# The lead-in of a hybrid attention and SSM layer: x transposed once, three weight slices behind the first adaLN pair

## The chip, the core and the metric

The kernel runs on one NeuronCore of one Trainium2 chip. The metric is device time in microseconds. Before the change the median of three runs was 1358.09 us (1357.22 to 1360.01).

## The reference

One layer of a streaming encoder for two groups of frames that share their weights: 512 new frames of a prompt and 64 frames of a sample (a cache of 512 keys stands before these). Only the start matters here:

```python
mod = (jax.nn.silu(c) @ w_ada + b_ada)[:, None, :]          # w_ada: 1024 x 6144
sh1, sc1, gt1, sh2, sc2, gt2 = jnp.split(mod, 6, axis=-1)
h = rms_normalize(x) * g_norm_mix * (1.0 + sc1) + sh1       # x: 576 x 1024
q, k, v, qi, ki, wi, z, xbc, dt, gate_logits = jnp.split(h @ w_in, offs, axis=-1)
```

Everything else (sparse attention with an indexer, a Mamba-2 scan, the merge of both branches, a SwiGLU FFN) comes from h @ w_in and from x itself, which is needed again for the residual.

## The kernel before

**Layout.** h is kept transposed, model channels on the 128 partitions: eight tiles (kt = 0 to 7) of 128 channels by 576 frames (512 of the prompt, 64 of the sample). Matmuls are made of three products of fp32r halves: a high part (`hTh`, `wh`) and a low part (`hTl`, `wl`), high times high, low times high, high times low. A weight slice of 512 KB is loaded to `raw` (two buffers), split by ScalarE into `wh` and by VectorE into `wl` (three buffers each).

**The lead-in.** x comes in five blocks of up to 128 frames (`xt`). ScalarE squares each with a sum over the row; 1/rms follows on VectorE and GpSimd (`rs`). VectorE scales the block (`xn`), TensorE transposes it with the identity in eight pieces (`px<-ident,xn`), ScalarE copies it to `xnT`. Apart from this, TensorE also transposes x itself (`mm<-ident,xt`), VectorE copies that to `xs`, and it is stored to `x_d` for the residual.

The adaLN shift and scale come in four pairs (`ada_pair`): pair j loads 256 columns of shift and 256 of scale weights (four loads of 512 KB, `adr`, eight buffers), and TensorE makes two groups of 32 small matmuls (`py<-adr,sil`), one per half of the model channels. The result is copied (`ra`), transposed, given its bias (`modc`) and made into A1 = (1 + scale) * g. Then `h_tile` makes two tiles of h: `hu` = xnT * A1 + shift (even tiles on VectorE, odd ones on ScalarE), `hTh` a copy of hu on ScalarE, `hTl` = hu - hTh (VectorE, for two tiles GpSimd).

Three weight slices are used while h comes into being: one called misc (104 columns: indexer keys, head weights, dt; its product is in an `mm` buffer with 104 columns) and two gate slices (an `mm` buffer, and the two halves in `px` and `py`). For each tile of h there are six matmuls with each. The first full weight use behind them is the first indexer query projection, `mm<-wh,hTh` with 256 columns, whose two slices are the fourth and fifth.

**What sets the order.** The program is written in its natural order and recorded as a list of operations. A planner (`Plan.order`) gives each a cost in time and a priority, its place in the program less an offset (`R.prio`), and runs a list schedule: the engine that is free first takes the ready operation with the lowest priority number. The instructions are then emitted in that order on each engine. All lines of the profile are therefore one line, 534, and work is told apart by tile names. Each load is issued on SyncE's queue (SP), in the planned order; the program uses eight DMA semaphores in turn, so that a load waits for the one eight places ahead of it. `EARLY` says how many weight slices may have been asked for after each pair.

Of the kernel before, what the change touches and what calls it, by code (L numbers as in the profile page):

```python
# [248 lines left out]
class Plan:  # L249
# [142 lines left out]
    def order(self):  # L392
# [50 lines left out]
        while n < len(ops):  # L443
# [98 lines left out]
def build(tc, I, O):  # L542
# [74 lines left out]
    def fetch(done, limit=1 << 30):  # L617
# [6 lines left out]
        with R.prio(4000 if done or limit > 99 else 0):  # L624
            more = True
            while more:
                more = False
                j = state["ld"]
                if j < min(len(queue), limit) and j < state["sp"] + NRAW:
                    i, s = queue[j]  # L630
                    if s == "misc":
                        raw = wp.tile([P, 8, 104], F32, name="rawm", tag="raw", bufs=NRAW)
# [3 lines left out]
                    else:  # L636
                        raws[j] = (load_raw(*s), s[1], s[2], 27 <= j < 48)
# [184 lines left out]
    pool.memset(rs, 1.0)  # L822
    for tb in range(5):
# [11 lines left out]
    rowsD = sp.tile([48, P], F32, name="rowsD")  # L835
    sync.dma_start(rowsD, I["b_ada"][0].rearrange("(a b) -> a b", b=P))
    badc = cp.tile([P, 48], F32, name="badc")
    t = px("pbadc")
    pe.transpose(t[:, :48], rowsD, ident[:48, :48])
    vec.tensor_copy(badc, t[:, :48])  # L840
    rowsA = sp.tile([64, P], F32, name="rowsA")
    for r0, n, src in ((0, 8, I["g_norm_mix"][0]), (8, 8, I["g_norm_ffn"][0]), (16, 16, I["g_ssm_norm"][0]), (32, 32, I["b_conv"][0])):
        sync.dma_start(rowsA[r0:r0 + n], src.rearrange("(a b) -> a b", b=P))
# [43 lines left out]
    with R.prio(-1500):  # L887
        for tb in range(5):
# [1300 lines left out]
```

## Time and profile before

| | |
|---|---|
| median of 3 runs | 1358.09 us |
| the profiled execution, its own time | 1358.19 us |
| span from first to last instruction | 1356.4 us |
| mean granted TensorE clock | 0.999 |
| TensorE busy | 1335.1 us, 98% |
| VectorE, ScalarE, GpSimd busy | 1130.7, 737.3, 241.5 us |
| loaded and stored | 200.02 MB, 147 GB/s in the mean |

A row of the timeline gives start and length in us, engine, operation, and what is written from what; in square brackets the idle time of the engine before it and what ended this. A matmul's length is from its start to its modelled end, so neighbours overlap, and the distance of their starts is what one costs. PE is TensorE, PEld its weight loads, DVE VectorE, ACT ScalarE, POOL GpSimd, SP and SPq SyncE with its queue.

### The profile page before, as it was taken

The page shows a single profiled execution, that of the slowest core. Times are in us where ns is not written, and L with a number is a line of the kernel's source. Part 1 is how long each engine was busy: PE and PEld are TensorE (multiplying, and loading weights), DVE is VectorE, ACT ScalarE, POOL GpSimd, SP SyncE. Part 2 cuts the span into 40 slices and gives each one's busy share as a digit, 9 for nine tenths or more (in the row PEclk, how much of TensorE's full clock was granted, in tenths as well). Part 3 has the DMA queues.
Part 4 walks back from the last instruction along what each step waited for, and adds up shares of the span by engine and source line. Part 5 has one row for each costly group of instructions (what it writes and reads, how often), then busy time and mean ns, then how long its engine had stood idle before and what let it go on. Part 6 is the DMA issues. An engine that isn't in the chain of part 4 may idle for free.

```text
span 1356.4 us, 27609 instructions
## 1 busy us (share of the span) xinstructions
PE 1335.1 (98%) x10651; PEld 1298.5 (96%) x10651; DVE 1130.7 (83%) x2238; ACT 737.3 (54%) x1515; POOL 241.5 (18%) x370
## 2 busy tenths in 40 slices
PE   7999999999999999999999999999999999999998
PEld 5899999999999999999999999999999999999998
DVE  4688999887777798888887688858799998868997
ACT  5445343787777666666565342225576555564543
POOL 1212011230301235545453300001000000000000
PEclk9999999999999999999999999999999999999999
DMA  9862335674754464455445698748333433334423
GB/s 292 235 176 88 101 115 140 142 176 116 165 143 119 131 185 114 115 149 136 135 112 175 212 300 252 232 143 260 98 94 110 125 103 89 98 101 130 133 73 87
DMA packets 268370, 200.02 MB, mean 147 GB/s; under 512 B 25168, under 2 KB 240368, under 8 KB 268240
## 3 DMA queue, kind: packets, MB, share of 16 engines
q1 hardware_dynamic: 264288, 184.11, 46.4%
q0 software_dynamic: 3952, 14.16, 5.1%
q8 instruction: 83, 1.36, 0.4%
q14 instruction: 47, 0.39, 0.1%
HBM read 158.27 MB, written 28.96 MB: 138 GB/s over the span
## 4 chain that ended last, share of the span: by engine, by line
PE 82%; DVE 10%; DMA 3%; ACT 1%; issue 1%; POOL 1%; SPq 1%; DVEq 0%; ACTq 0%; POOLq 0%
PE mm L534 56%; PE py L534 14%; PE px L534 11%; DVE score L534 3%; DVE m L534 2%; DVE wl L534 2%; DMA raw<-in_w_in 1%; SPq L534 1%; DMA xt<-in_x_sample 1%; DMA raw<-in_w_down 0%; ACT wh L534 0%; DMA rawb<-in_w_down 0%; DMA rowsB<-in_w_conv 0%; DVE cu L534 0%; DVE tok L534 0%
## 5 line engine op out<-in xcount | busy, mean ns | idle before, releaser
L534 ACT ACTIVATE wh<-raw 128x1024 fp32r<-128x1024 f32 (+3 forms) x146 | 142.3, 978 | 182.5 <-PE mm L534 125.8
L534 PE MATMUL mm<-hTh,wh 128*128 128x288 f32 (+1 forms) x1024 | 230.3, 302 | 0.5 <-ACT hTh L534 0.5
L534 PE MATMUL mm<-hTl,wh 128*128 128x288 f32 (+1 forms) x1024 | 230.7, 300 | 0.0
L534 PE MATMUL mm<-hTh,wl 128*128 128x288 f32 (+1 forms) x1024 | 229.2, 300 | 0.5 <-DVE wl L534 0.5
L534 PEld LDWEIGHTS mm<-hTh,wh 128*128 128x128 f32 (+1 forms) x1024 | 165.8, 188 | 4.0 <-ACT hTh L534 1.3
L534 PEld LDWEIGHTS mm<-hTl,wh 128*128 128x128 f32 (+1 forms) x1024 | 166.4, 188 | 2.4 <-issue 0.9
L534 PEld LDWEIGHTS mm<-hTh,wl 128*128 128x128 f32 (+1 forms) x1024 | 165.1, 188 | 2.5 <-issue 1.1
L534 DVE TENSOR_TENSOR wl<-raw,wh 128x1024 fp32r<-128x1024 f32 (+2 forms) x102 | 123.4, 1211 | 28.5 <-ACT wh L534 24.3
L534 DVE SCALAR_TENSOR_TENSOR cu<-xc,wc,cu 128x579 f32<-128x579 f32 x96 | 83.2, 868 | 2.0 <-ACT cu L534 1.0
L534 PE MATMUL mm<-wh,hTl 128*128 128x256 f32 x256 | 72.6, 284 | 0.0
L534 PE MATMUL mm<-wl,hTh 128*128 128x256 f32 x256 | 72.1, 282 | 0.0
L534 PE MATMUL mm<-wh,hTh 128*128 128x256 f32 x256 | 71.9, 283 | 0.0
L534 DVE SCALAR_TENSOR_TENSOR aacc<-adr,sil,aacc 128x512 f32<-128x512 f32 x84 | 59.1, 752 | 4.3 <-DMA adr<-in_w_ada 4.3
L534 PE MATMUL mm<-yh,wl 128*128 128x288 f32 x256 | 55.2, 296 | 0.0
L534 PE MATMUL mm<-yh,wh 128*128 128x288 f32 x256 | 55.0, 296 | 0.0
L534 PE MATMUL mm<-yl,wh 128*128 128x288 f32 x256 | 54.9, 296 | 0.0
L534 PE MATMUL mm<-xhS,wh 128*128 128x290 f32 (+1 forms) x248 | 54.7, 295 | 0.0
L534 ACT ACTIVATE P<-lg,mn 128x128 f32<-128x128 f32 (+4 forms) x72 | 41.8, 581 | 23.5 <-DVE mn L534 22.1
L534 PE MATMUL mm<-xhS,wl 128*128 128x290 f32 (+1 forms) x232 | 51.1, 295 | 0.0
L534 ACT ACTIVATE dec<-dec,nacs 128x128 f32<-128x128 f32 x128 | 42.4, 393 | 15.4 <-POOL dec L534 15.4
L534 PEld LDWEIGHTS mm<-wh,hTl 128*128 128x128 f32 x256 | 48.4, 189 | 0.4
L534 PEld LDWEIGHTS mm<-wh,hTh 128*128 128x128 f32 x256 | 48.0, 188 | 0.6 <-issue 0.4
(553 smaller groups left out, 3993.2 us busy)
## 6 DMA issues: line engine op xcount, KB each, us to landing
raw<-in_w_in SPq DMA_DIRECT2D x80, 512.0 KB, 4.0
adr<-in_w_ada SPq DMA_DIRECT2D x36, 512.0 KB, 5.1
raw<-in_w_gate_up SPq DMA_DIRECT2D x22, 512.0 KB, 4.0
wl<-raw POOLq DMA_DIRECT2D x21, 512.0 KB, 5.1
rawu<-in_w_gate_up SPq DMA_DIRECT2D x20, 512.0 KB, 3.9
bc<-acs_d SPq DMA_DIRECT2D x32, 256.0 KB, 3.4
raw<-in_w_branch_ssm SPq DMA_DIRECT2D x16, 512.0 KB, 4.9
gate_d<-sg SPq DMA_DIRECT2D x16, 288.0 KB, 2.1
```

The source lines that it names most:

```text
L534: getattr(engines[x.eng], x.fn)(*[real(a) for a in x.args], **{k: real(v) for k, v in x.kw.items()})
```

## The change

- x itself is transposed as each block comes in, into `xT` (576 frames by 8 tiles); nine of the ten copies are on VectorE, one on ScalarE. `x_d` is stored from `xT`, in four stores.
- 1/rms is transposed and spread over the partitions by TensorE (five transposes of a broadcast column), and VectorE multiplies `xT` by it to give `xnT`, in five products. The scaled blocks `xn`, their 40 transposes and their copies are gone.
- The bias rows and gain rows (`rowsD`, `rowsA`) are transposed while x still comes in.
- The first three weight slices have raw buffers of their own, and `EARLY` asks for all three behind pair 0; the fourth is asked for after pair 3.
- `h_tile`: ScalarE makes hTh straight from xnT (scale and shift in the same instruction, in two parts); VectorE makes hu and hTl for all tiles.
- In the planner, the load rate of SyncE's queue in the first 60 us is 335 in place of 360 (thousand bytes per us), and the first seven weight loads have no priority offset.

```diff
-                dma_free = max(queue + 1.3, dma_free) + op.bytes / 360e3
+                dma_free = max(queue + 1.3, dma_free) + op.bytes / (335e3 if at < 60.0 else 360e3)
...
-    def load_raw(src, nk, n):
-        raw = wp.tile([P, nk, n], F32, name=f"raw{cnt[0]}", tag="raw", bufs=NRAW)
+    def load_raw(src, nk, n, own=0):
+        if own:
+            raw = sp.tile([P, nk, n], F32, name=f"rawe{cnt[0]}_{own}")
+        else:
+            raw = wp.tile([P, nk, n], F32, name=f"raw{cnt[0]}", tag="raw", bufs=NRAW)
...
-                if j < min(len(queue), limit) and j < state["sp"] + NRAW:
+                if j < min(len(queue), limit) and (j < 3 or j < max(state["sp"], 3) + NRAW):
                     i, s = queue[j]
+                    at = R.offset
+                    R.offset = 0 if j < 7 else at
...
+    xT = xsp.tile([P, 8, T], F32, name="xT")
     for tb in range(5):
         n = P if tb < 4 else NS
+        p = pmm(f"pxt{tb}")
+        for kt in range(8):
+            pe.transpose(p[:, kt // 4, (kt % 4) * P:(kt % 4) * P + n], xt[tb][:n, kt * P:(kt + 1) * P], ident[:n, :n])
         xn = sp.tile([P, D], F32, name=f"xn{tb}", tag="xn", bufs=2)
         act.activation(xn[:n], xt[tb][:n], AF.Square, accum_out=rs[:n, tb:tb + 1])
         rstd_of(rs[:n, tb:tb + 1], rs[:n, tb:tb + 1], 1, n, D)
-        vec.tensor_scalar(xn[:n], xt[tb][:n], rs[:n, tb:tb + 1], None, op0=OP.mult)
         for k4 in range(2):
-            p = px(f"pxn{tb}_{k4}")
-            for j in range(4):
-                kt = 4 * k4 + j
-                pe.transpose(p[:, j * P:j * P + n], xn[:n, kt * P:(kt + 1) * P], ident[:n, :n])
-            act.activation(xnT[:, 4 * k4:4 * k4 + 4, tb * P:tb * P + n], p.rearrange("p (k q) -> p k q", k=4)[:, :, :n], AF.Copy)
+            d, src = xT[:, 4 * k4:4 * k4 + 4, tb * P:tb * P + n], p[:, k4].rearrange("p (k q) -> p k q", k=4)[:, :, :n]
+            if 2 * tb + k4 in (1,):
+                act.activation(d, src, AF.Copy)
+            else:
+                vec.tensor_copy(d, src)
...
+    pr = px("prs"), pairs_bank[:, 2 * P:3 * P]
+    for tb in range(5):
+        pe.transpose(pr[tb // 4][:, tb % 4 * P:tb % 4 * P + P], rs[:, tb:tb + 1].to_broadcast([P, P]), ident)
+    vec.tensor_tensor(xnT[:, 0:2, 0:NP_], xT[:, 0:2, 0:NP_], pr[0][:, None, :].to_broadcast([P, 2, NP_]), OP.mult)
+    vec.tensor_tensor(xnT[:, :, NP_:T], xT[:, :, NP_:T], pr[1][:, None, :NS].to_broadcast([P, 8, NS]), OP.mult)
+    for k in range(2, 8, 2):
+        vec.tensor_tensor(xnT[:, k:k + 2, 0:NP_], xT[:, k:k + 2, 0:NP_], pr[0][:, None, :].to_broadcast([P, 2, NP_]), OP.mult)
...
         for s, c0, n in PARTS:
-            if kt % 2:
-                act.activation(u[:, c0:c0 + n], xnT[:, kt, c0:c0 + n], AF.Identity, bias=sh1[:, kt, s:s + 1], scale=A1[:, kt, s:s + 1])
-            else:
-                vec.tensor_scalar(u[:, c0:c0 + n], xnT[:, kt, c0:c0 + n], A1[:, kt, s:s + 1], sh1[:, kt, s:s + 1], op0=OP.mult, op1=OP.add)
-        act.activation(hTh[:, kt, :], u, AF.Copy)
-        (pool if kt % 4 == 1 else vec).tensor_tensor(hTl[:, kt, :], u, hTh[:, kt, :].bitcast(F32), OP.subtract)
-
-    EARLY = [1, 2, 3, 3]
+            act.activation(hTh[:, kt, c0:c0 + n], xnT[:, kt, c0:c0 + n], AF.Identity, bias=sh1[:, kt, s:s + 1], scale=A1[:, kt, s:s + 1])
+            vec.tensor_scalar(u[:, c0:c0 + n], xnT[:, kt, c0:c0 + n], A1[:, kt, s:s + 1], sh1[:, kt, s:s + 1], op0=OP.mult, op1=OP.add)
+        vec.tensor_tensor(hTl[:, kt, :], u, hTh[:, kt, :].bitcast(F32), OP.subtract)
+
+    EARLY = [3, 3, 3, 4]
...
-    with R.prio(-1500):
-        for tb in range(5):
...
+    for hf in range(2):
+        xst.append((x_d[:, :, hf, 0:HP], xT[:, :, HP * hf:HP * hf + HP]))
+        xst.append((x_d[:, :, hf, HP:TH], xT[:, :, NP_ + HS * hf:NP_ + HS * hf + HS]))
```

Three places of the planned order show what moves. The first is SyncE's queue from pair 1 on; before (adr_4 to adr_7 at the top are pair 1, the next four pair 2, the last four pair 3; the 128x8x128 slices are the two gate slices, 128x4x256 the first one of the query projection):

```order
L534 DMA adr_6_167<-in_w_ada 128x4x256
L534 DMA adr_7_168<-in_w_ada 128x4x256
L534 DMA raw_1_85<-in_w_in 128x8x128
L534 DMA adr_0_161<-in_w_ada 128x4x256
L534 DMA adr_1_162<-in_w_ada 128x4x256
L534 DMA adr_2_163<-in_w_ada 128x4x256
L534 DMA adr_3_164<-in_w_ada 128x4x256
L534 DMA raw_1_85<-in_w_in 128x4x256
L534 DMA raw_0_84<-in_w_in 128x8x128
L534 DMA adr_4_165<-in_w_ada 128x4x256
L534 DMA adr_5_166<-in_w_ada 128x4x256
L534 DMA adr_6_167<-in_w_ada 128x4x256
```

and now, from the end of pair 0:

```order
L534 DMA adr_3_160<-in_w_ada 128x4x256
L534 DMA rawm_0_165<-in_w_in 128x8x72
L534 DMA rawm_0_165<-in_w_in 128x8x32
L534 DMA rawe1_1_0_166<-in_w_in 128x8x128
L534 DMA rawe2_2_0_167<-in_w_in 128x8x128
L534 DMA adr_4_161<-in_w_ada 128x4x256
```

The gate slices have moved ahead of pair 1; the query slice stands behind pair 3, where it was ahead of it.

The second is ScalarE between the end of x's part and the first h tiles, before (raw_0 to wh_0 is the misc slice):

```order
L534 ACTIVATE wh_0_86<-raw_0_84 128x832
L534 ACTIVATE xnT_0_153<-px_0_97 128x4x64
L534 ACTIVATE xnT_0_153<-px_1_98 128x4x64
L534 ACTIVATE hu_1_170<-xnT_0_153,modc_0_74,A1_0_117 128x512
L534 ACTIVATE hu_1_170<-xnT_0_153,modc_0_74,A1_0_117 128x64
L534 ACTIVATE hTh_0_131<-hu_0_169 128x576
```

and now:

```order
L534 ACTIVATE wh_0_84<-rawm_0_165 128x832
L534 ACTIVATE wh_1_85<-rawe1_1_0_166 128x1024
L534 ACTIVATE hTh_0_131<-xnT_0_149,modc_0_74,A1_0_117 128x512
L534 ACTIVATE hTh_0_131<-xnT_0_149,modc_0_74,A1_0_117 128x64
L534 ACTIVATE wh_2_86<-rawe2_2_0_167 128x1024
L534 ACTIVATE hTh_0_131<-xnT_0_149,modc_0_74,A1_0_117 128x512
```

The high part of the first h tile no longer waits for hu, and stands behind the split of the second slice; the third slice's split stands between the first two h tiles.

The third is TensorE behind the last adaLN group (`mm` with wh_1 and wl_1 is the first gate slice, `px` and `py` with wh_2 and wl_2 the second), before:

```order
L534 MATMUL mm_0_99<-hTh_0_131,wl_1_90 128x288 x2
L534 MATMUL mm_0_99<-hTh_0_131,wh_1_87 128x288 x2
L534 MATMUL mm_0_99<-hTl_0_132,wh_1_87 128x288 x2
L534 MATMUL py_1_96<-ident_0_71,ra_1_108 128x128
L534 MATMUL mm_0_99<-hTh_0_131,wl_1_90 128x288 x2
L534 MATMUL py_0_95<-hTh_0_131,wl_2_91 128x288
L534 MATMUL px_0_97<-ident_0_71,rowsB_0_159 128x128
L534 MATMUL px_1_98<-hTh_0_131,wh_2_88 128x288
```

and now:

```order
L534 MATMUL mm_1_98<-hTh_0_131,wl_0_87 104x288 x2
L534 MATMUL mm_0_97<-hTl_0_132,wh_1_85 128x288 x2
L534 MATMUL mm_0_97<-hTh_0_131,wl_1_88 128x288 x2
L534 MATMUL py_1_96<-ident_0_71,ra_1_108 128x128
L534 MATMUL mm_0_97<-hTh_0_131,wh_1_85 128x288 x2
L534 MATMUL mm_0_97<-hTl_0_132,wh_1_85 128x288 x2
L534 MATMUL px_0_99<-ident_0_71,rowsB_0_155 128x128
L534 MATMUL mm_0_97<-hTh_0_131,wl_1_88 128x288 x2
L534 MATMUL py_0_95<-hTl_0_132,wh_2_86 128x288
```

Between this group and the query projection stand 75 matmuls of the three slices before and 68 now; the rowsB transpose comes after 9 of them before and after 10 now.

More of the change, by code (lines that the diff above doesn't have):

```diff
@@ L636, in fetch @@
                     else:
-                        raws[j] = (load_raw(*s), s[1], s[2], 27 <= j < 48)
+                        raws[j] = (load_raw(*s, own=j if j < 3 else 0), s[1], s[2], 27 <= j < 48)
+                    R.offset = at
                     state["ld"] += 1
@@ L822, in build @@
     pool.memset(rs, 1.0)
+    rowsD = sp.tile([48, P], F32, name="rowsD")
+    rowsA = sp.tile([64, P], F32, name="rowsA")
+    badc = cp.tile([P, 48], F32, name="badc")
+    vc = cp.tile([P, 64], F32, name="vc")
+    sync.dma_start(rowsD, I["b_ada"][0].rearrange("(a b) -> a b", b=P))
+    for r0, n, src in ((0, 8, I["g_norm_mix"][0]), (8, 8, I["g_norm_ffn"][0]), (16, 16, I["g_ssm_norm"][0]), (32, 32, I["b_conv"][0])):
+        sync.dma_start(rowsA[r0:r0 + n], src.rearrange("(a b) -> a b", b=P))
+    xT = xsp.tile([P, 8, T], F32, name="xT")
     for tb in range(5):
         n = P if tb < 4 else NS
+        p = pmm(f"pxt{tb}")
+        for kt in range(8):
+            pe.transpose(p[:, kt // 4, (kt % 4) * P:(kt % 4) * P + n], xt[tb][:n, kt * P:(kt + 1) * P], ident[:n, :n])
         xn = sp.tile([P, D], F32, name=f"xn{tb}", tag="xn", bufs=2)
@@ L835, in build @@
[L835 to L843, printed above, removed]
+            d, src = xT[:, 4 * k4:4 * k4 + 4, tb * P:tb * P + n], p[:, k4].rearrange("p (k q) -> p k q", k=4)[:, :, :n]
@@ new lines, in build @@
+            if 2 * tb + k4 in (1,):
+                act.activation(d, src, AF.Copy)
+            else:
+                vec.tensor_copy(d, src)
+        if tb == 2:
+            t = px("pv")
+            pe.transpose(t[:, 0:48], rowsD, ident[:48, :48])
+            pe.transpose(t[:, 64:128], rowsA, ident[:64, :64])
+            vec.tensor_copy(badc, t[:, 0:48])
+            vec.tensor_copy(vc, t[:, 64:128])
+    pr = px("prs"), pairs_bank[:, 2 * P:3 * P]
+    for tb in range(5):
+        pe.transpose(pr[tb // 4][:, tb % 4 * P:tb % 4 * P + P], rs[:, tb:tb + 1].to_broadcast([P, P]), ident)
@@ L847, in build @@
-    t = px("pv")
-    pe.transpose(t[:, :64], rowsA, ident[:64, :64])
-    vec.tensor_copy(vc, t[:, :64])
     g_mix, g_ffn = vc[:, 0:8], vc[:, 8:16]
@@ L886, in build @@
     xst = []
-    with R.prio(-1500):
-        for tb in range(5):
-            n = P if tb < 4 else NS
-            p = pmm(f"pxt{tb}")
-            for kt in range(8):
-                pe.transpose(p[:, kt // 4, (kt % 4) * P:(kt % 4) * P + n], xt[tb][:n, kt * P:(kt + 1) * P], ident[:n, :n])
-            st = xsp.tile([P, 8, P], F32, name=f"xs{tb}", tag="xs", bufs=5)
-            for k4 in range(2):
-                vec.tensor_copy(st[:, 4 * k4:4 * k4 + 4, :n], p[:, k4].rearrange("p (k q) -> p k q", k=4)[:, :, :n])
-            if tb < 4:
-                xst.append((x_d[:, :, tb // 2, tb % 2 * P:tb % 2 * P + P], st))
-            else:
-                for hf in range(2):
-                    xst.append((x_d[:, :, hf, HP:TH], st[:, :, HS * hf:HS * hf + HS]))
+    for hf in range(2):
+        xst.append((x_d[:, :, hf, 0:HP], xT[:, :, HP * hf:HP * hf + HP]))
+        xst.append((x_d[:, :, hf, HP:TH], xT[:, :, NP_ + HS * hf:NP_ + HS * hf + HS]))
     sync.dma_start(rowsB, I["w_conv"][0].rearrange("j (a b) -> (j a) b", b=P))
```

3 lines of the change are left out of this document (1 added, 2 removed).

## The prediction

> **What bounds the kernel now.** I read the engine totals first, then a table of the span by stage, then the start row by row on TensorE (PE), VectorE (DVE) and ScalarE (ACT).
>
> ```profile
> PE 1335.1 (98%) x10651; PEld 1298.5 (96%) x10651; DVE 1130.7 (83%) x2238; ACT 737.3 (54%) x1515; POOL 241.5 (18%) x370
> core 0: us, PE busy (x) PEld busy (x) DVE busy (x) ACT busy (x) POOL busy (x), PEclk, DMA share, GB/s
> 5.00:20.00 15.00, 12.33 (x116) 10.88 (x120) 9.08 (x19) 9.07 (x18) 2.51 (x5) 1.00 1.06 302
> 20.00:25.00 5.00, 3.45 (x73) 2.44 (x63) 3.64 (x12) 3.46 (x7) 0.28 (x1) 0.98 1.07 344
> 25.00:28.00 3.00, 3.00 (x32) 1.78 (x30) 0.76 (x1) 0.76 (x2) 1.42 (x1) 0.50 1.16 319
> 28.00:45.40 17.40, 15.70 (x216) 12.85 (x208) 7.46 (x17) 7.55 (x12) 1.42 (x1) 0.99 1.02 313
> 45.40:57.30 11.90, 11.06 (x82) 10.54 (x83) 9.71 (x15) 6.82 (x13) 7.02 (x11) 1.00 0.61 146
> 57.30:150.00 92.70, 91.94 (x789) 90.33 (x788) 83.16 (x153) 39.73 (x77) 14.98 (x9) 1.00 0.48 137
> 150.00:400.00 250.00, 248.04 (x1848) 240.79 (x1848) 209.05 (x529) 153.44 (x306) 47.70 (x44) 1.00 0.56 140
> 400.00:800.00 400.00, 399.47 (x3334) 384.67 (x3333) 329.41 (x644) 245.13 (x575) 155.67 (x265) 1.00 0.53 151
> 800.00:1356.40 556.40, 549.83 (x4196) 544.01 (x4194) 478.08 (x851) 269.87 (x507) 8.95 (x20) 1.00 0.46 138
> ```
>
> From 57.3 us on PE is idle for 0.76 + 1.96 + 0.53 + 6.57 = 9.8 us out of 1299: it is the bound. Before that the loads are: DMA share 1.0 or more from 5 to 45 us, at 302 to 344 GB/s. So the change is worth what it moves the moment at which PE starts the first query projection (`mm<-wh,hTh`, 57.32 us), minus what the rest gives back.
>
> ```profile
> 19.73 1.08 PE L534 MATMUL py<-adr,sil 128*32 128x128 f32 x32
> 26.77 2.04 PE L534 MATMUL py<-adr,sil 128*32 128x128 f32 x32
> 41.30 0.29 PE L534 MATMUL px<-hTh,wl 128*128 128x288 f32 x1
> 41.52 1.08 PE L534 MATMUL py<-adr,sil 128*32 128x128 f32 x32
> 42.53 0.51 PE L534 MATMUL mm<-hTl,wh 128*104 128x288 f32 x2
> 44.30 1.08 PE L534 MATMUL py<-adr,sil 128*32 128x128 f32 x32
> 47.72 0.33 PE L534 MATMUL px<-ident,rowsB 128*128 128x128 f32 x1 [0.84 <-DMA rowsB<-in_w_conv]
> 54.01 0.40 PE px L534 x3
> 57.32 0.37 PE L534 MATMUL mm<-wh,hTh 128*128 128x256 f32 x1
> ```
>
> The adaLN pairs (eight half-pair groups of 32 `py<-adr,sil` matmuls) are taken as their loads come in. The last group ends at 45.38; then 11.94 us pass to 57.32. A full-clock h matmul costs 0.132 us (three in 0.40), a group 1.1 us (41.30 + 0.13 to 42.53).
>
> **The loads.**
>
> ```profile
> 33.03 4.23 SPq L534 DMA_DIRECT2D adr<-in_w_ada  x4
> adr<-in_w_ada SPq DMA_DIRECT2D x16, 512.0 KB, 6.7
> 24.20 1.38 PE L534 MATMUL py<-adr,sil 128*32 128x128 f32 x28 [0.86 <-DMA adr<-in_w_ada]
> 3.43 8.58 DMA xt<-in_x_sample
> ```
>
> The last pair's loads are issued by 37.26 and take 6.7: landing about 43.9, and PE takes them at 44.30. Ahead of them the queue now holds four weight slices, in the changed one only three; the first query slice moves behind. That is 0.52 MB at 0.32 MB/us: 1.6 us earlier, 42.3. But two slices of 0.52 MB move ahead of pair 1, which is waited for at 24.20: 3.2 us later, about 27.4 and 30.5 for its halves; pair 2 about 33.5 and 36.7 (one slice later than now), pair 3 about 40 and 42.3. The loads stay saturated: each reused adaLN buffer is asked for with some 2 MB (6 us) still under way.
>
> **x and the norm** (5 to 20 us).
>
> ```profile
> L534 PE MATMUL px<-ident,xn 128*128 128x128 f32 x32 | 4.7, 295 | 1.3 <-DVE rs L534 1.3
> L534 DVE TENSOR_SCALAR xn<-xt,rs 128x1024 f32<-128x1024 f32 x4 | 3.0, 746 | 0.3 <-POOL rs L534 0.3
> L534 DVE TENSOR_TENSOR wl<-raw,wh 128x1024 fp32r<-128x1024 f32 x4 | 5.4, 1356 | 1.7 <-ACT wh L534 1.7
> 18.34 1.05 ACT L534 ACTIVATE xn<-xt 64x1024 f32<-64x1024 f32 x1
> 20.31 0.75 DVE L534 TENSOR_SCALAR xn<-xt,rs 64x1024 f32<-64x1024 f32 x1 [0.66 <-POOL rs L534]
> 66.42 0.69 DVE L534 TENSOR_TENSOR kis<-px,kis 128x512 fp32r<-128x512 f32 x1 [0.16 <-ACT kis L534]
> 20.98 0.28 DVE L534 COPY ra<-py 128x128 f32<-128x128 f32 x1
> ```
>
> 40 transposes of xn go (the 32 large ones 4.7 us of PE), five of 1/rms come; five DVE scalings (3.7 us) go. The products that replace them (four of 128x1024 with a PSUM operand, one of 128x512) have no row: from below the weight subtraction, 1.23 alone (1.36 in the mean), from above twice 0.69 = 1.38; I take 1.3, so 4 x 1.3 + 0.69 = 5.9 us. The last x block lands at 12.0 and needs 1.97 from its square to the first use of 1/rms (18.34 to 20.31): they run from 14.0 to about 20. Pair 0 needs DVE at 20.98 (`ra`), so this is hidden, with 1 us of cover. I count it at nothing; without the cover it would delay the first h tile by that much, which PE's waits for pairs 1 and 2 absorb.
>
> **First h tile.** ACT writes h's high part from xnT itself, so one ACT pass falls away:
>
> ```profile
> 23.41 0.77 DVE L534 TENSOR_SCALAR hu<-xnT,A,modc 128x512 f32<-128x512 f32 x2
> 29.08 1.06 ACT L534 ACTIVATE wh<-raw 128x1024 fp32r<-128x1024 f32 x1 [3.33 <-DMA raw<-in_w_in]
> 39.26 0.80 ACT L534 ACTIVATE hu<-xnT,modc,A 128x512 f32<-128x512 f32 x1
> ```
>
> But ACT's order now puts the split of the second slice ahead of it. That slice stands where pair 1's first load stands now, so it lands between 23 and 24.2; plus 1.06 and 0.80 the first h matmul comes at 24.9 to 26.1, now 25.51. I take 25.0: no gain here.
>
> **25 us to the end of the last adaLN group.** By the listing 76 of the 144 h matmuls of the three early slices stand ahead of it (now 69): 76 x 0.132 = 10.0, six groups 6.6, transposes 0.4, together 17.0: 42.0 at full clock and with no wait. The clock was 0.50 between 25 and 28 (a group took 2.04 in place of 1.08); PE is emptier before 25 than now, so I take the same stretch again, 1.6 us more: 43.6. Waits for pairs 1 and 2 and for new h tiles: 1.0, one wait of the size of the 0.86 (a late pair) and 0.84 (rowsB) above. That gives 44.6, now 45.38. Below: the landing, 42.3 + 1.1 = 43.4. Above: a second half-clock stretch, 46.2.
>
> **From there to the query projection.**
>
> ```profile
> 46.79 0.16 DVE L534 SCALAR_TENSOR_TENSOR A<-modc,vc 128x4 f32<-128x4 f32 x1
> 49.24 2.49 DVE L534 TENSOR_TENSOR hTl<-hu,hTh 128x576 fp32r<-128x576 f32 x2 [0.23 <-ACT hTh L534]
> 40.67 0.76 DVE L534 TENSOR_TENSOR hTl<-hu,hTh 128x576 fp32r<-128x576 f32 x1
> 49.21 2.91 POOL L534 TENSOR_TENSOR tabs<-cs,gqk 128x320 f32<-128x320 f32 x3
> ```
>
> Now 75 h matmuls are left: 75 x 0.132 = 9.9, the transposes 0.7, the wait for rowsB 0.84 and 0.5 of others make the 11.94. In the changed program 68 are left: 9.0 + 0.7 + 0.5 = 10.2. The rowsB wait goes: its load is queued behind one weight slice fewer. What is late next is the last low part on DVE. A1 comes 1.57 us after the group (45.38 to 46.95), the last hTl after hu twice (1.54), hTl twice (1.52) and one 0.29: 4.9 us after the group. By the listing PE has 33 h matmuls and three transposes (4.8 us) ahead of it, just enough. Beside POOL's rope tables an hTl took 1.24 in place of 0.76, twice: up to 1.0 us later, and I take half, 0.5. So 10.7, between 9.7 (no other waits) and 11.7.
>
> The Trainium skill, page "SBUF — State Buffer", section "SBUF: two separate sides", says that a DVE instruction with two SBUF inputs and a GpSimd instruction lock each other out for a whole instruction. By that rule each of the two hTl could wait about 1 us and the term would be up to 2.0; the rows show 0.48 each.
>
> **Sum.** 44.6 + 10.7 = 55.3 against 57.32: 2.0 us. Best 43.4 + 9.7 = 53.1 (4.2 us), worst 46.2 + 11.7 = 57.9 (0.6 lost). x_d's stores only become fewer and wider; they wait for no engine on the path and I count them at nothing (DMA is half idle there, share 0.48). DVE's first `aacc` also comes some 2 us sooner, so DVE does not hold PE back more than now. In the second half PE's two listings agree row for row. The profiled execution took 1358.19 (span 1356.4 and 1.8 around it), 0.1 above the median of 1358.09: so the end moves to 1356.2 by it and to 1358.09 - 2.0 = **1356.1** by the median, which I give.
>
> **Rivals.**
>
> *PE runs cold twice.* In the changed order PE has one transpose between the end of pair 0 (now 20.8) and 25.0; now it is busy 3.45 us of 20 to 25, and the clock still fell to 0.50 for 3 us. If the low stretch lasts twice as long, 1.6 us are lost, and with the last hTl late by the full 1.0 the start moves to 56.2 + 1.2 = 57.4: no change, 1358.2. Against: the h matmuls at half clock fill PE from 25 on, and the same filling ended the stretch at 28. The Trainium skill, page "TensorE: Matmul & The Clock Gate", section "What's actually happening", has the clock halved after an idle window of about 3.4 us and back after a busy one, at a free-running phase. The row's 0.50 over 3 us agrees; by that rule an idle stretch of over 4 us always costs one, and the phase decides on a second. Chance 0.2.
>
> *The loads alone decide.* PE stays at full clock or catches up, and takes the last pair as it lands: 53.1 to 54, 3.3 to 4.2 us, 1354.3. For: PE followed the landing within 0.4 us now (43.9 and 44.30). Against: the sum above leaves only 0.4 us for it at full clock. Chance 0.2.
>
> *The middle gives more back (slower).* Up to about 45% of PE's list the planner's order differs. There PE's waits are for DVE's rope sums:
>
> ```profile
> PE py L534 <- DVE tok L534: 1.8, 2, 1.1
> L534 DVE TENSOR_TENSOR tok<-tok,tmpb x6: 1479/1488/1493, 81.5 to 364.9; 128x1280 f32<-128x1280 f32 x6
> ```
>
> Six such sums feed PE's transposes; two make it wait now. If the new order puts adaLN column sums ahead of all six, each costs up to 1.1 us: 6.6 - 1.8 = 4.8 more, less 2.0 gained: 1361.0. It decides from two further waits on. Against: in the new listing the first rope's sum comes with fewer rows ahead of it than now. Chance 0.13.
>
> The rest, 0.47, is the forecast. **Numbers.** A measurement of this kernel tells about 0.2% (2.7 us) from no change; the three runs spread over that much. Faster by more: all of the second rival and a little over a third of the forecast, 0.38. Slower by more: most of the third, 0.11. Within: 0.51. The range holds the forecast with its bounds and most of the second rival below, the first above, and half of the third is left out: 1352.8 to 1359.6.
>
> **What would show it.** Right: the last adaLN group ends between 43.4 and 46.2; `mm<-wh,hTh` starts between 53 and 56.5; no wait for rowsB; PE clock 0.50 in one 3 us stretch between 18 and 31; PE idle from there to the end within 2 us of 9.8. Wrong: the query projection starts later than 57, or waits for its own weights (ACT `wh`, DVE `wl`); PE's idle after it grows past 12 us; or the start gains over 4.2 us, which would mean that the loads were not the limit.

## The result, and the profile after

| | before | changed |
|---|---|---|
| median | 1357.99 us (4 runs, 1357.22 to 1360.01) | 1368.13 us (4 runs, 1367.71 to 1370.84) |
| ratio, 95% interval | | 1.0071 (1.0059 to 1.0084) |
| profiled execution | 1358.19 us, span 1356.4 | 1370.84 us, span 1368.9 |

The change makes the kernel 10 us slower; forecast were 2 us less. The profiled execution of the changed kernel lies 2.7 us above its median, so its trace shows some 12.5 us of loss where the median has 10. Three single executions of the runs below took far longer than all others of their kernels (3351.03 us, the one that the trace of `lead_warm` shows, 4581.93 of `lead_late` and 1438.91 of `lead_late_warm32`), and no ratio uses them.

The table of the span by stage, of the changed kernel (columns as before: busy time of each engine, PE clock, DMA share):

```profile
5.00:20.00 15.00, 11.03 (x47) 8.24 (x47) 7.08 (x17) 6.63 (x12) 2.78 (x5) 1.00 1.10 315
57.30:150.00 92.70, 92.15 (x791) 90.57 (x790) 73.85 (x130) 40.27 (x78) 19.46 (x11) 1.00 0.48 139
150.00:400.00 250.00, 247.40 (x1845) 240.18 (x1844) 214.18 (x539) 147.86 (x298) 46.88 (x41) 1.00 0.57 142
400.00:800.00 400.00, 393.73 (x3259) 375.96 (x3259) 325.77 (x641) 245.16 (x578) 158.51 (x268) 1.00 0.49 139
800.00:1400.00 600.00, 561.10 (x4282) 555.23 (x4280) 489.51 (x867) 274.65 (x514) 8.94 (x20) 1.00 0.45 135
```

From 57.3 us on TensorE is now idle for 0.55 + 2.60 + 6.27 us up to 800 (before 0.76 + 1.96 + 0.53), and 568.9 - 561.1 = 7.8 from there to the end of the span: 17.2 where it was 9.8. Most of this growth, 5.7 of 7.4 us, is between 400 and 800, in the scan (xw, xc and dec below are its tiles). The waits of TensorE:

```profile
PE py L534 <- DVE xw L534: 3.5, 3, 2.4
PE mm L534 <- ACT xc L534: 1.5, 1, 1.5
```

(total, times, longest, from 57 to 752 us). Neither stood in the list before. The longest wait, 2.43 us up to 668.5, costs more than its own length, for TensorE ran at half speed behind it. One stretch of the table, before and then now:

```profile
660.00:680.00 20.00, 20.00 (x164) 19.51 (x164) 17.07 (x29) 11.43 (x26) 10.26 (x16) 1.00 0.55 146
```
```profile
660.00:680.00 20.00, 17.57 (x128) 16.89 (x128) 13.56 (x22) 8.76 (x22) 3.79 (x13) 0.91 0.51 156
```

The trace's record of the clock has half speed from 668.4 to 671.8, which is 1.7 us lost. So of the 11.4 us that this execution loses behind the query projection, the added idle time shows 7.4 and this stretch 1.7; the rest, some 2 us, stands in no wait that the profile lists. And the start, row by row on TensorE:

```profile
10.25 0.69 PE L534 MATMUL mm<-ident,xt 128*128 128x128 f32 x2 [0.79 <-DVE rs L534]
10.94 1.49 PE L534 MATMUL mm<-ident,xt 128*128 128x128 f32 x6
20.84 3.64 PE L534 MATMUL py<-adr,sil 128*32 128x128 f32 x64 [1.50 <-DVE xnT L534]
27.03 1.29 PE L534 MATMUL mm<-hTh,wh 128*104 128x288 f32 x4 [1.64 <-ACT hTh L534]
30.33 0.69 PE L534 MATMUL mm<-hTh,wh 128*104 128x288 f32 x2
31.42 1.94 PE L534 MATMUL py<-adr,sil 128*32 128x128 f32 x32
47.67 1.08 PE L534 MATMUL py<-adr,sil 128*32 128x128 f32 x32
50.21 0.27 PE L534 MATMUL px<-ident,rowsB 128*128 128x128 f32 x1
58.40 0.37 PE L534 MATMUL mm<-wh,hTh 128*128 128x256 f32 x1
```

The first h matmul comes at 27.03 (25.51 before), the last group ends at 48.69 (45.38), the query projection starts at 58.40 (57.32). So the lead-in loses 1.1 us instead of gaining 2.0, and the remaining 9 to 11 us are lost behind it, by work that the change does not touch.

### The profile page after: what moved, and what is told of

Read it like the earlier page. It is cut to its first block, busy times and chain, and to the rows that moved or that the text cites. A ratio compares the mean times of both kernels' runs of the same rounds, so it can differ in the third digit from the quotient of the medians.

```text
span 1368.9 us, 27561 instructions
## 1 busy us (share of the span) xinstructions
PE 1339.8 (98%) x10616; PEld 1299.5 (95%) x10616; DVE 1136.5 (83%) x2247; ACT 731.9 (53%) x1506; POOL 243.8 (18%) x368
## 4 chain that ended last, share of the span: by engine, by line
PE 74%; DVE 11%; DMA 6%; ACT 4%; issue 3%; POOL 1%; SPq 0%; DVEq 0%; ACTq 0%; POOLq 0%
PE mm L534 50%; PE py L534 14%; PE px L534 10%; DVE wl L534 2%; DMA bc<-acs_d 2%; DVE score L534 1%; DMA wl<-raw 1%; DVE m L534 1%; DMA raw<-in_w_in 1%; ACT wh L534 1%; DVE cu L534 1%; DMA raw<-in_w_down 1%; DVE fg L534 0%; DVE dlS L534 0%; ACT dec L534 0%
## 5 line engine op out<-in xcount | busy, mean ns | idle before, releaser
L534 ACT ACTIVATE wh<-raw 128x1024 fp32r<-128x1024 f32 (+2 forms) x143 | 139.1, 976 | 171.8 <-PE mm L534 126.0
L534 DVE TENSOR_TENSOR wl<-raw,wh 128x1024 fp32r<-128x1024 f32 (+1 forms) x99 | 119.8, 1212 | 28.6 <-ACT wh L534 26.8
L534 PEld LDWEIGHTS mm<-wl,hTh 128*128 128x128 f32 x256 | 48.1, 188 | 1.1 <-DVE wl L534 0.6
```

The source lines that it names most:

```text
L534: getattr(engines[x.eng], x.fn)(*[real(a) for a in x.args], **{k: real(v) for k, v in x.kw.items()})
```

## The experiments

To part the lead-in from what stands behind it, the planner can be held to a list: an operation recorded behind the second gate slice is handed to its engine's queue only when it is the next one of a list written into the kernel, taken from the planned order of another kernel. Lead-in operations are placed as always. Held to its own list the changed kernel keeps its rows: in `after_bc3`, the last run below, all 2247 of VectorE come in the order that they have in the changed kernel.

```diff
     fillers(NE)
+    R.cut, R.loose = len(R.ops), set()
...
-            heapq.heappush(future[op.eng], (t, op.prio, op.i))
+            rest.push(op, t)      # kept back until it is the next of its engine's list REST
```

Below, "old order" and "new order" are the lists of the kernel before and of the changed kernel. Ratios are to the kernel before on the same chip.

### Lead-in and order exchanged

Two kernels: the changed lead-in with the old order, and the old lead-in with the new order.

> The changed lead-in, with everything recorded behind the two gate slices issued on each engine in the row order of the kernel before. Theory A (the planner's new order of the middle costs some 10 us, the lead-in itself 1.1 us): the query projection starts near 58.4 us, the gap to the kernel before stays near 1.1 us to the end, 1359.2 us (1358 to 1361). Theory B (the changed lead-in slows the middle directly, whatever the order: buffers elsewhere, stores of x_d, another phase): 1366 to 1369 us. In between, near 1363: each has a part.

Measured: 1364.08 us, 1.0039 (1.0026 to 1.0052).

> The lead-in of the kernel before, with the rest issued in the row order of the changed kernel. Theory A: the query projection starts near 57.3 us, and some 10 us are lost between 57 and 740 us, above all between 455 and 740: 1367 us (1364 to 1370). Theory B: 1358 us, within 2 us.

Measured: 1363.66 us, 1.0039 (1.0024 to 1.0054). Each has about half of the loss, so neither theory holds alone. For the first kernel, the trace shows where its part beyond the 1.1 us of the lead-in arises, in one place:

```profile
101.70 0.48 PE L534 MATMUL py<-ident,tok 128*128 128x128 f32 x1 [3.40 <-DVE tok L534]
```
```profile
98.83 1.42 DVE L534 SCALAR_TENSOR_TENSOR aacc<-adr,sil,aacc 128x512 f32<-128x512 f32 x2 [5.67 <-DMA adr<-in_w_ada]
100.16 1.48 DVE L534 TENSOR_TENSOR tok<-tok,tmpb 128x1280 f32<-128x1280 f32 x1
```
```profile
83.45 1.31 SPq L534 DMA_DIRECT2D x_d<-xT  x2
87.34 0.54 SPq L534 DMA_DIRECT2D x_d<-xT  x1
89.70 1.62 SPq L534 DMA_DIRECT2D adr<-in_w_ada  x1
```

The rope sum (`tok`) stands on VectorE behind an adaLN column sum (`aacc`); this waits 5.67 us for its load, and the load stands on SyncE behind two stores of x_d of 1 MB each (the changed lead-in has four wider stores where the old list has six, so they had no place in it and were placed freely). Here too the clock record has half speed behind the wait, from 101.3 to 104.8. So this cost belongs to the stores in this mixed order, not to the lead-in.

### The lead-in's own price

```diff
-    for hf in range(2):
-        xst.append((x_d[:, :, hf, 0:HP], xT[:, :, HP * hf:HP * hf + HP]))
-        xst.append((x_d[:, :, hf, HP:TH], ...))
+    for tb in range(4):
+        xst.append((x_d[:, :, tb // 2, tb % 2 * P:tb % 2 * P + P], xT[:, :, tb * P:tb * P + P]))
+    for hf in range(2):
+        xst.append((x_d[:, :, hf, HP:TH], ...))
```

and the six stores at the places that the old order has for them.

> As the run with the changed lead-in and the old row order, but x_d is stored in the six pieces and at the six places of the kernel before, so that SyncE's rows behind the lead-in are the old ones too. If the wait of 3.4 us at 101.7 us came from the 1 MB stores ahead of an adaLN load: that wait falls to the 0.7 us of the kernel before, the gap to it stays at 1.1 us, 1359.9 us. If it came from the later start itself (VectorE behind): the wait stays, 1364 us.

Measured: 1360.11 us, 1.0009 (0.9998 to 1.0020). The longest wait for `tok` is 0.9 us, where it was 3.40, and the projection starts at 58.44. The lead-in by itself costs 1.2 us by this ratio, which can't be told from nothing, and the old order would have kept the rest.

The same stores with the new order, all else as in the changed kernel:

> The changed kernel in its own row order, x_d stored in six pieces in place of four. If the 1 MB stores have a part in the loss: 1364 to 1366. If not: 1367 to 1370.

Measured: 1367.15 us, 1.0060 (1.0047 to 1.0073), against 1.0071 (1.0059 to 1.0084) with the wide stores. In the changed kernel itself the stores have no part that can be told from nothing.

### Which part of the change

Each part alone, on the kernel before, with the old order behind it and x_d in six pieces.

```diff
 only_slices:  own=j if j < 3 else 0;  EARLY = [3, 3, 3, 4];  335e3 if at < 60.0;  R.offset = 0 if j < 7
 only_x:       xT transposed once, rs spread by TensorE, xnT = xT * rs on VectorE
 only_h:       act.activation(hTh[...], xnT[...], bias=sh1, scale=A1); hu and hTl on VectorE
```

> The kernel before with the change's loads alone (three early slices in buffers of their own behind pair 0, the fourth behind pair 3, the two planner numbers); x, norm and h_tile as before, everything behind the gate slices in the old row order. Theory x (the loss in the lead-in comes from x's part: TensorE cold and VectorE's products late): the loads bring what was predicted of them, the query projection starts 1 to 2 us earlier than before, 55.3 to 56.3, total 1357. Rival (the loads cost: pair 1 now comes 3 us later and TensorE waits for it): start at 58 or later, 1360.

> The kernel before with x's part alone (x transposed once, 1/rms spread, products on VectorE, x_d in the six old pieces), old row order behind. Theory x: TensorE runs at half clock through x's blocks, VectorE's products end near 24, the first h matmul comes 1.5 to 2 us later than the 25.5 before, the projection starts at 58.5 to 60, total 1360 to 1361. Rival: start within 0.5 us of 57.3, 1358.6.

> The kernel before with h_tile alone changed (high part straight from xnT on ScalarE, both others on VectorE), old row order behind. All theories: the first h matmul up to 0.8 us earlier, the projection within 0.7 us of 57.3, total 1358 to 1359.

Measured: 1359.85 us, 1.0008 (0.9999 to 1.0018); 1360.30 us, 1.0007 (0.9998 to 1.0017); 1358.34 us, 1.0001 (0.9992 to 1.0011). The times are too close to tell apart; the traces tell more. The start of the projection, one row from each:

```profile
57.44 0.37 PE L534 MATMUL mm<-wh,hTh 128*128 128x256 f32 x1
```
```profile
59.60 0.37 PE L534 MATMUL mm<-wh,hTh 128*128 128x256 f32 x1
```
```profile
55.50 0.37 PE L534 MATMUL mm<-wh,hTh 128*128 128x256 f32 x1
```

Against 57.32: the loads +0.1, x's part +2.3, h's part -1.8. Each is one trace. Three further traces with the old lead-in unchanged start at 58.51 (with the new order behind it), 56.59 and 56.11 (order_att_new and order_ssm_new below), so a single start is good to about 1.2 us; the changed lead-in is steadier, from 58.34 to 58.84 in five traces. So x's part loses and h's part gains by more than this scatter, but not by much, and the times don't confirm it. A part of h's gain is TensorE's speed: the clock record of this trace has no half-speed stretch near 25 us, where the kernel before has one of 3.4 us (1.7 us lost). The loads bring nothing: in the trace of only_slices TensorE waits 4.10 us for the first h tile, which stands behind slice splits on both engines (the third slice's high part on ScalarE, 25.63 to 26.67; a low part on VectorE, 25.31 to 26.53, between the two parts of hu), and what the loads gain later only makes up for it.

### Why x's part loses

VectorE (DVE) of the changed kernel:

```profile
18.06 0.76 DVE L534 COPY xT<-mm 128x256 f32<-128x256 f32 x2 [0.41 <-PE mm L534]
18.73 1.21 DVE L534 TENSOR_TENSOR xnT<-xT,px 128x1024 f32<-128x1024 f32 x1
20.11 0.68 DVE L534 TENSOR_TENSOR xnT<-xT,py 128x512 f32<-128x512 f32 x1
20.70 3.47 DVE L534 TENSOR_TENSOR xnT<-xT,px 128x1024 f32<-128x1024 f32 x3
24.57 0.29 DVE L534 COPY ra<-py 128x128 f32<-128x128 f32 x1 [0.23 <-PE py L534]
```

and TensorE from 9 to 12 us, the kernel before and then the changed one, in the columns of the tables by stage:

```profile
9.00:12.00 3.00, 3.00 (x20) 3.00 (x19) 2.47 (x5) 0.69 (x2) 0.56 (x1) 1.00 1.04 185
```
```profile
9.00:12.00 3.00, 2.21 (x11) 1.81 (x10) 1.44 (x3) 3.00 (x7) 0.57 (x1) 1.00 1.08 245
```

with two rows of the kernel before:

```profile
7.38 3.04 PE L534 MATMUL mm<-ident,xt 128*128 128x128 f32 x13 [0.79 <-DVE rs L534]
11.55 1.26 PE L534 MATMUL mm<-ident,xt 128*128 128x128 f32 x10
```

Three things meet. A block of x now takes 2.97 us (10.25 to 13.21): eight transposes at 0.24, and a wait of 0.78 for VectorE. VectorE's products therefore begin at 18.7, and the last three (3.47 us) stand ahead of the copy ra, which opens the way to the first h tile. Pair 0's sums on TensorE come as late: they wait 1.50 us for the product at 20.11, which reads other columns of their PSUM buffer, and ra waits 0.23 us for them. And TensorE works at half speed: an h matmul takes 0.24 us until 33.3, then 0.13. The kernel before starts at half speed too (13 transposes in 3.04 us, 0.23 each), but there the transposes of xn fill the waits for the copies: TensorE is busy from 7.7 to 11.2 us without a gap, and behind that ten transposes take 1.26 us. Without them it is busy for 2.21 of 3 us, and stays at half speed to 33.5. The single parts agree: only_x has half speed up to 24.9, only_slices and only_h up to 11.0 and 10.9. Three remedies on the lead-in with six stores:

```diff
 lead_bank:       pr = px("prs"), pairs_bank[:, 2 * P:3 * P]  ->  px("prs"), pc0[:, 2 * P:3 * P]
 lead_warm:       pe.transpose(<spare PSUM>, ident, ident): 32 ahead of x, 4 behind each block,
                  16 ahead of pair 0, 14 behind its transpose
 lead_warm_bank:  both
```

> The former, with 78 transposes of the identity that nobody reads, laid into TensorE's empty places (32 ahead of x, 4 behind each block, 16 ahead of pair 0, 14 behind its transpose). Theory clock (the removed transposes of xn had kept TensorE's clock up; without them it runs at half clock from 9 to 33 us, where the first h matmuls and one group lose 3 us): x's transposes take 0.12 in place of 0.25 us each, the first h matmul comes at 25 to 26, the query projection starts at 55 to 56, 2 to 3 us below the former run. Rival (the slow start is in the loads or on VectorE): the start moves by less than 0.7 us.

Measured: 1359.47 us, 1.0012 (1.0002 to 1.0022), against 1.0009 of lead_six, so the 2 to 3 us less did not come. Its trace does not show a usual start, so where the projection begins isn't known.

> As the first of these, with the sample's spread 1/rms in another PSUM bank than pair 0's sums. Theory bank: pair 0's first group no longer waits 1.5 us for VectorE, and all behind it comes 1.5 us earlier, query projection at 56.9. Theory clock or VectorE: the copy ra stands behind three products on VectorE until 24.1 anyway, so the start moves by 0.5 us at most.

Measured: 1359.44 us, 1.0010 (1.0000 to 1.0020); projection at 58.18. Pair 0's sums are 1.7 us earlier, but ra does not come earlier:

```profile
19.44 3.60 PE L534 MATMUL py<-adr,sil 128*32 128x128 f32 x64
24.77 0.33 PE L534 MATMUL py<-ident,ra 128*128 128x128 f32 x1 [1.72 <-DVE ra L534]
```

The wait has only changed its place, from the bank to VectorE's products: theory bank falls.

> Both. Theory clock: as the warm run, and up to 1 us more since the products now come earlier: query projection at 54 to 55.5, total 1355 to 1357, below the kernel before. If the last adaLN loads (landing near 42.3) set the end of the lead-in, it cannot come below 53.1.

Measured: 1358.99 us, 1.0005 (0.9995 to 1.0014); projection at 56.80, later than the 54 to 55.5 that were expected. Its TensorE:

```profile
12.03 0.82 PE L534 MATMUL mm<-ident,xt 128*128 128x128 f32 x6
19.48 3.34 PE L534 MATMUL mm<-ident 128*128 128x128 f32 x16
27.31 0.85 PE L534 MATMUL mm<-hTh,wh 128*104 128x288 f32 x4 [0.26 <-ACT hTh L534]
30.15 0.43 PE L534 MATMUL mm<-hTh,wh 128*104 128x288 f32 x2
```

Six transposes take 0.82 in place of 1.49 us and h matmuls run at 0.13 from the first on. The first one comes no earlier, since VectorE's products still stand ahead of ra (and the 16 filling transposes ahead of pair 0, at half speed again, take 3.34 us); the start gains 1.6 us over lead_six (58.44 to 56.80) and 1.4 over lead_bank, which differs by the filling alone. These are TensorE's speed, by one trace each; the times of the three can't be told apart. The next kernels, which have the other bank too, move the products:

```diff
-    for k in range(2, 8, 2):
-        vec.tensor_tensor(xnT[:, k:k + 2, 0:NP_], xT[:, k:k + 2, 0:NP_], pr[0]..., OP.mult)
...
+        lo = h_tile(2 * j + 1)
+        if j < 3:
+            k = 2 * j + 2
+            with R.after([lo]):
+                vec.tensor_tensor(xnT[:, k:k + 2, 0:NP_], ...)
```

> The changed lead-in, old row order behind (six pieces of x_d), the sample's 1/rms in the other bank, and the three products for tiles 2 to 7 taken out of VectorE's row ahead of pair 0's copy ra: each stands behind the low parts of the pair of tiles before it. Theory VectorE (the products hold ra and with it the first h tile): the copy ra comes as pair 0's sums end, near 23, the first h matmul near 25.2 in place of 26.9 to 27.3, projection at 56.5, 1358. If TensorE's clock alone sets the lead-in: first h earlier, but half clock to 33 or later, projection at 57.8 to 58.4, 1359 to 1360.

Measured: 1359.23 us, 1.0002 (0.9993 to 1.0012). As theory VectorE has it, ra's transpose comes at 22.91 and the first h matmul at 25.03, with TensorE at half speed from 25.3 to 32.1; projection at 57.26, between what the two theories gave, and 0.9 earlier than with the other bank alone (58.18). VectorE's products are worth 1.9 us at the first h tile, and 0.9 of it arrives, again by one trace each.

> The same with transposes of the identity in TensorE's empty places (13 ahead of x, 4 behind each block, 4 ahead of pair 0, 10 behind its transpose). Both causes: x's blocks end 1.5 us earlier, first h matmul near 23.5 to 24.5 at full clock, projection at 53.5 to 55, 1355 to 1356, below the kernel before. If the loads of the adaLN pairs set the rest: not below 53.1.

Measured: 1359.57 us, 1.0001 (0.9987 to 1.0016), with 12 runs from 1354.93 to 1364.51. With 13 filling transposes ahead of x the profiled execution stayed at half speed to 26.9 us, and then the four behind each block cost time themselves (a block took 3.8 us); the projection starts at 60.43, where 53.5 to 55 were expected. A filling that does not reach full speed is a load like any other.

```diff
-    13 ahead of x, 4 behind each block, 4 ahead of pair 0, 10 behind its transpose
+    32 ahead of x, 4 behind each block, 0 ahead of pair 0, 10 behind its transpose
```

> As the warm run with late products, with 32 filling transposes ahead of x in place of 13 and none ahead of pair 0. With the 32, the earlier run was at full clock in x's blocks; then x's part ends near 19.3, pair 0's sums near 21.5, the first h matmul comes near 24 at full clock, the projection near 53.5 to 54.5, 1355 to 1356, below the kernel before by 0.2%. If the loads or VectorE's other work set it: 56 to 57, 1358.

Measured: 1357.59 us, 0.9991 (0.9981 to 1.0000).

```profile
1.68 5.71 PE L534 MATMUL py<-ident 128*128 128x128 f32 x32 [1.68 <-POOL ident L534]
12.27 0.82 PE L534 MATMUL mm<-ident,xt 128*128 128x128 f32 x6
19.72 3.47 PE L534 MATMUL py<-adr,sil 128*32 128x128 f32 x64
25.75 0.85 PE L534 MATMUL mm<-hTh,wh 128*104 128x288 f32 x4 [0.69 <-ACT hTh L534]
55.86 0.37 PE L534 MATMUL mm<-wh,hTh 128*128 128x256 f32 x1
```

TensorE is at full speed from 5.8 us up to pair 0 and again from 22.9, and the projection starts at 55.86 (the expected 53.5 to 54.5 were missed by 1.4: pair 0's sums took 3.47 us and the first h tile came at 25.75). The whole is 1.2 us below the kernel before, at the edge of what can be told. By the ratios it is 0.8% (11 us) below the changed kernel, with the same change in it: its lead-in repaired, and the old order behind.

### The order by itself

One number of the planner, with no work added or taken away: in the kernel before 335 for 360, in the changed kernel 360 for 335.

```diff
-                dma_free = max(queue + 1.3, dma_free) + op.bytes / 360e3
+                dma_free = max(queue + 1.3, dma_free) + op.bytes / (335e3 if at < 60.0 else 360e3)
```

> The kernel before with one number of the planner changed (load rate 335 in place of 360 in the first 60 us): no work is added or removed, only the row order is dealt anew. Theory A (the time hangs on the order that is dealt): the middle moves by several us, most likely upward, 1360 to 1375 us, with the lead-in within 1 us of the kernel before. Theory B: no change, 1356 to 1361 us.

> The changed kernel with that number put back to 360: the same work, another deal. Theory A: the middle moves by several us in either direction, 1356 to 1376 us, at least 3 us away from the changed kernel's 1368. Theory B: 1366 to 1370 us, as the changed kernel.

Measured: 1373.36 us, 1.0105 (1.0089 to 1.0121), and 1374.19 us, 1.0107 (1.0089 to 1.0126). Both are as the first theory has it. The first of them starts the projection at 57.46, as before, and loses some 14 us behind it: a number that changes no work costs more than the whole change. All the other orders tried here are slower than that of the kernel before; whether that one is unusually good can't be told from so few.

Then the new order in one stage alone, on the kernel before: up to about 450 us (attention), or from there on (the scan).

```diff
-REST = old order
 order_att_new:  +REST = new order up to the border, old order from there
 order_ssm_new:  +REST = old order up to the border, new order from there
```

> The kernel before with the changed kernel's row order behind the lead-in up to about 450 us, and its old order from there. If the order's cost adds up over the stages: 4.9 - 2.2 = 2.7 us, 1361 to 1362, of it up to 1 at the start and the rest in waits between 80 and 330 us. If the two stages work on each other: 1358.9 to 1360.

> The kernel before with its old row order up to the end of attention (about 450 us), and from there the row order of the changed kernel. If the order's loss of 5 us sits in the SSM stretch: nothing is lost up to 450, 3 to 4 us between 490 and 740 (TensorE waiting for VectorE's xw), 1362 to 1363 us. If it is set up in attention and only shows later: 1359 to 1360.

Measured: 1360.17 us, 1.0012 (1.0002 to 1.0021), and 1361.12 us, 1.0021 (1.0011 to 1.0030). Each lies between the ranges of its two theories. Together they make 1.0033 where both at once had 1.0039, so within the intervals the stages add up. In all traces the same matmul (of a kind, the k-th) can be found; its start, less that in the trace before, in us:

```
                        projection   480 us   740 us   span
changed                    +1.1       +3.3    +11.5   +12.5
new_six                    +1.5       +4.0     +8.5    +8.9
old lead-in, new order     +1.2       +3.0     +8.7    +8.4
new lead-in, old order     +1.0       +5.0     +5.7    +5.6
lead_six                   +1.1       +1.1     +1.4    +0.1
order_att_new              -0.7       +1.9     +1.6    +2.4
order_ssm_new              -1.2       -1.2     +3.5    +2.9
before_rate335             +0.1      +10.7    +15.0   +14.0
```

The new order loses 1.8 to 2.6 us between the projection and 480, and 4.5 to 8.2 between 480 and 740, whatever the lead-in. The old order with six stores (lead_six) loses at most 0.3 there; with the four wide stores it loses the 4.0 at 101 us. Behind 740 no more than 1.0 is added; TensorE's rows before and now agree from 665 us on.

### A suspected cause within the scan

In the changed kernel the longest wait of TensorE (2.43 us at 668) hangs on a chain that begins on SyncE: SyncE's queue, GpSimd, ScalarE, VectorE, TensorE.

```profile
649.30 8.32 SPq L534 DMA_DIRECT2D bc<-acs_d  x2
658.27 0.53 SPq L534 DMA_DIRECT2D bc<-acs_d  x1
```
```profile
653.04 1.97 POOL L534 TENSOR_TENSOR r<-r,mhalf 128x10 f32<-128x10 f32 x1
654.98 2.27 POOL L534 TENSOR_TENSOR cs<-bc,bcx 128x512 f32<-128x512 f32 x1
664.61 0.41 POOL L534 TENSOR_SCALAR_AFFINE_SELECT decS<-bc 64x256 f32<-64x256 f32 x1 [6.48 <-DMA bc<-acs_d]
```
```profile
665.05 0.59 ACT L534 ACTIVATE decS<-decS,nacs 64x64 f32<-64x64 f32 x2 [5.65 <-POOL decS L534]
665.55 1.04 ACT L534 ACTIVATE wh<-raw 128x1024 fp32r<-128x1024 f32 x1
```
```profile
666.62 1.22 DVE L534 TENSOR_TENSOR wl<-raw,wh 128x1024 fp32r<-128x1024 f32 x1 [2.69 <-ACT wh L534]
668.00 0.42 DVE L534 TENSOR_TENSOR xw<-px,wst 128x256 f32<-128x256 f32 x1 [0.16 <-ACT bt L534]
```

The second of two loads of bc is held from 649 to 657: both buffers are in use until GpSimd has made cs, and GpSimd has r (1.97) in its row ahead of that. In the kernel before r stands at 645.66 and the same two loads are through in 1.58 us. So the queue is held, the last chunk's load lands late, ScalarE waits with a weight split behind it, and xw comes late. The same hold of 8.32 us stands in the traces of new_six and of the old lead-in with the new order, with waits for xw of 2.71 and 1.85 us behind it. The trial: a third buffer.

```diff
-        bc = sd.tile([P, 4, P], F32, name=nm + "bc", tag="bc", bufs=2)
+        bc = sd.tile([P, 4, P], F32, name=nm + "bc", tag="bc", bufs=3)
```

(with two small output tiles put into the buffers of bt, to make room)

> The changed kernel, each engine's rows in its own order, with one change: three buffers in place of two for bc (the decay rows that SyncE loads for each chunk of the scan). If that buffer is what the new order makes SyncE wait for: no stall of 8 us on SyncE at 649 us, GpSimd's wait for bc and TensorE's 2.4 us at 668 go, 3 to 4 us less than the changed kernel's 1368, 1364 to 1365. If the wait only moves on to the next load or to VectorE: 1367 to 1369.

Measured: 1367.32 us, 1.0063 (1.0047 to 1.0080). The stall on SyncE is gone, and nothing is gained:

```profile
650.23 1.08 SPq L534 DMA_DIRECT2D bc<-acs_d  x2
```
```profile
PE py L534 <- DVE xw L534: 2.8, 2, 1.4
PE px L534 <- DVE dec L534: 1.3, 1, 1.3
```

TensorE now waits 1.4 us for xw in two places and 1.3 for dec in a third. So the wait moved on, as the second theory has it, and this buffer is not what the new order's loss hangs on. Other places were not tried, and what it would take to mend the order was not found.

## Why the prediction was wrong

**What bounds the kernel** was read rightly: behind the lead-in TensorE is the bound, with 9.8 us of idle time. The conclusion drawn from it, that the change is worth what it moves the query projection, holds only if the rest stays as it is.

**The step that failed most** is the sentence in the sum, "so DVE does not hold PE back more than now", with the listings' agreement in the second half put beside it. The listings differed up to 45% of TensorE's rows (in the traces the rows differ up to the 5305th of 10651, at 665 us), and that stretch was priced at nothing in the forecast. The new order alone costs 4.9 us with the old lead-in, and a new order with no change of work costs 14.5. A wait also costs more than its length where half speed follows, as the 1.7 us behind 668 show; the prediction looked for half speed in the lead-in alone. The third rival had the sign and the place of its cause (the planner's order in the middle), but the wrong mechanism: VectorE's rope sums held TensorE for 1.8 us before, and now for 0.4 in one place; what waits is the scan, for xw and xc, of which the prediction said nothing. Its 1361.0 was 7 us short and its chance of 0.13 much too low. A trace of the kernel before does not hold the new order, so it could not give this price.

**x and the norm, counted at nothing**: failed. The price of the products was right (1.21, 0.68 and 3.47 for three, 5.4 in all, where 5.9 were taken). Their place was wrong: they were put from 14.0 to 20, with the last block's landing as their start, and ran from 18.7 to 24.2, because transposes and copies of a block take 2.97 us in turn. The cover of 1 us did not do: ra came at 24.57 where 20.98 was allowed, 3.6 late.

**First h tile at 25.0**: measured 27.03. The split of the second slice on ScalarE, taken as the limit, was long done (ScalarE waited 4.05 us for A1); ra was late by the step above.

**25 us to the last group's end**, 19.6 forecast: measured 21.7 (27.03 to 48.69). In lead_warm_bank, at full speed, TensorE is busy for 18.8 us in the same rows, where 17.0 were summed; in the changed kernel for 21.5, so half speed cost 2.7 in place of 1.6; the wait of 1.0 did not come (0.2 of idle time). The prediction took half speed for one stretch that an idle time brings about. In the changed kernel's trace TensorE was not at full speed at all before 33.5, and the kernel before had started the same way, up to 11.2; its rows at 7.38 and 11.55 showed that. The rival "PE runs cold twice" came nearest for the lead-in: its start of 57.4 is 1.0 short of 58.40, and its price was that of two stretches, but not by its mechanism. Its sentence that an idle stretch of over 4 us always costs one is too simple. The recorded stretches are 3.41 us long, so an idle time must be nearly twice that to hold a whole one whatever its phase; and much shorter waits had half speed behind them: 2.43 us (668, changed kernel) and 1.85 us (666, the old lead-in with the new order), but not one of 2.71 us (668, new_six).

**The loads**: moved as described, but they set nothing. TensorE takes the last two groups (44.56, 47.67) with no wait for a load, and the loads alone start the projection at 57.44. The rival "the loads alone decide" falls.

**From there to the projection**, 10.7 forecast with 9.7 as lower bound: measured 9.71. rowsB is taken without a wait, as predicted, and the low parts beside GpSimd's tables held nobody.

**x_d's stores, counted at nothing**: right in the changed kernel as far as can be told (1.0060 against 1.0071), but only by luck of the order: in another one the 1 MB stores ahead of one load cost a wait of 3.4 us.

**What would show it wrong** was named rightly: projection later than 57, idle time above 12 us (it is 17.2).

One thing stays open. Lead-in alone (1.2 us) and order alone (5.3 by its ratio) make 6.5, both together 8.2 (new_six). The difference of 1.7 is within the intervals; whether the two work on each other was not settled.

## What to carry to other kernels

Where a planner sets the order of a whole program, a change at its start is two changes, the edit and the new order, and the second can be larger than the first. Price them apart: hold the rest of the program to its old row order and time the edit alone; then decide about the new order by measurement. And before work is taken out of an engine's idle stretch, look at what it kept going (here TensorE's speed, about 1.5 us) and at what is put in front of a short instruction that others wait for (three products ahead of one copy, 0.9 us); both prices are from single traces.

## What the runs showed of the hardware that was not expected

- TensorE's speed does not show in the PEclk column everywhere. In the changed kernel it reads 1.00 throughout the lead-in, while six transposes take 1.49 us and an h matmul 0.24; in the runs with 32 filling transposes the same rows take 0.82 and 0.13. The trace's record of the clock has its first entry at 33.5 us there (full speed), and the column counts the time ahead of the first entry as full. In the kernel before the first entry is at 11.2. The distance of starts is the surer sign.
- A partly busy TensorE did not come to full speed. In every trace that has such a record, its stretches inside the span last 3.41 us or a multiple of it. Cut into steps of this length, every change to full speed follows a step in which TensorE was busy for 89% or more. In the changed kernel the steps from 6.2 to 30.1 us were busy for 50 to 86%, and the next, busy throughout, brought full speed; in the kernel before it was the step from 7.7 to 11.2. Such a step was not always enough: one of 96%, in the changed kernel with the rate 360, was not. For the fall to half speed no such limit shows: a step of 66% led to it in the kernel before (21.4 to 24.8), and one of 63% (14.6 to 18.0) did not.
- The Trainium skill, page "TensorE: Matmul & The Clock Gate", section "What's actually happening", has half clock as the default, released by a busy window of about 3.4 us. The rows agree: 32 transposes at the start (5.71 us without a gap) released it, 13 did not in the profiled execution, and neither did a stretch with regular waits of 0.78 us.
- Two column ranges of one PSUM buffer were not independent: pair 0's matmuls waited 1.50 us for VectorE's reading of other columns, and not any more with the columns in another buffer. Whether the bank asks for that, or the way in which waits are set for a buffer, no run here tells.
